# Start of an even layer's input projection: channel blocks transposed when due and modulated by ScalarE from PSUM instead of by GpSimd

## The chip, the cores and the metric

One core of a Trainium2 chip runs one program. The metric is device time in microseconds (us) of one execution. TensorE (PE) multiplies and transposes from SBUF into PSUM, VectorE (DVE), ScalarE (ACT) and GpSimd (POOL) work on tiles, and SP's queue issues most DMAs. Each engine runs its own instructions in its own order and waits at semaphores for the others.

## What is computed

The program is a two-layer backbone over 1024 latent tokens of width 1024, with a context of 256 tokens. Only the start of the first (even) layer matters here:

```python
h_lat = modulate(x, shift, scale)   # layer_norm(x) * (1 + scale) + shift
...
gq_l, gk_l, gv_l, glr_l, gg_l, cq_l, ckv_l, kr_l, mg_l = proj(h_lat)   # h_lat @ w_in
```

Shift and scale are rows of silu(c) @ ada_w + ada_b. All is float32. A matmul of two float32 operands is made of three matmuls in a shorter format: each operand is split into a high part (a cast) and a low part (the operand minus its high part), and the products high x high, high x low and low x high are added in PSUM.

## The kernel before

The projection wants h transposed: eight blocks j of 128 channels, each 1024 tokens wide, worked in two halves of 512 tokens (x tiles 0 to 3 and 4 to 7, of 128 tokens each). The function `startup` loads and normalises x tiles (`load_norm`: statistics on VectorE, L207; three small operations on GpSimd, L198, L199 and L214; the normalisation on ScalarE, L239), reduces the modulation weights to a column of shift and one of scale for each block (`modulation`, L248, on VectorE, two loads of 512 KB per block), and splits six weight tiles (`weight`: load L301, high part on ScalarE L302, low part L305 on VectorE, or on GpSimd for the weights numbered in `PLO`, 2 and 4).

Before the loop it transposes all eight blocks of the first half at once (L361) into eight PSUM banks. Block 0 is modulated from its bank by ScalarE (L321); the other seven are copied to SBUF tiles xnT (L368, five by ScalarE, two by VectorE) and modulated there by GpSimd when their turn comes (L323). `part` makes the high part of h on ScalarE (L328) and the low part on VectorE (L329). `products(t, j)` adds the three matmuls of weight tile t and block j into the accumulator of tile t (helper lines L146, L147, L148); six accumulators take six of the eight PSUM banks, the other two serve the rest.

The order in which the steps are issued is written out by hand in a string:

```python
ORDER = "m w w r m w w r m w r m m x r x x x r m C s r s m s s r s s s s"
```

Here m is one block's modulation columns, w a weight, r a first-half block (modulate, split, products), x an x tile of the second half, s a second-half block (transposes L350, modulation, split; the low part is put off to the next step that calls `catch_up`), and C prepares the evictions and the first step of the context. The framework beneath issues an instruction as soon as it expects its inputs and a free buffer, earlier in the program first, so that the engines' orders follow this string only roughly; on the chip each engine's order is then fixed.

After the loop the six accumulators are evicted (`dup_ev`, L517 on ScalarE and L519 on VectorE, for four tiles; other copies for two), and a generator `rest` makes the second-half products of the six tiles. `in_proj_a` weaves it with the context's preparation (`startup_ctx`: 16 more loads and reductions of modulation weights, transposes L423, splits) and then multiplies four of the kept weights with the context (matmuls named chi and clo, 256 columns wide). All SBUF tiles of this stage come from one pool of 48 buffers, so that a load waits until a buffer is free.

Of the kernel before, what the change touches and what calls it, by code (L numbers as in the profile page):

```python
# [12 lines left out]
F32 = mybir.dt.float32  # L13
F32R = mybir.dt.float32r
I32 = mybir.dt.int32
AF = mybir.ActivationFunctionType
ALU = mybir.AluOpType
# [3 lines left out]
P = 128  # L21
# [3 lines left out]
KD = D // P  # L25
# [6 lines left out]
def f32(ap):  # L32
    return ap.bitcast(F32)


class Weights:
# [9 lines left out]
    def next(self):  # L46
        self.fill(1 + self.ahead)
        return self.q.pop(0)
# [184 lines left out]
def load_norm(k, src):  # L233

    nc = k.nc
    xt = k.b4(name="xt")
    nc.sync.dma_start(xt, src)
    r, nm = k.ln_stats(xt)
    nc.scalar.activation(out=xt, in_=xt, func=AF.Identity, scale=r, bias=nm)  # L239
    return xt  # L240
# [12 lines left out]
def silu_rows(k, c):  # L253

    nc = k.nc
    row, o = k.b4(F32, (1, D), name="crow"), k.b4(name="cB")
    nc.sync.dma_start(row, c)
    k.act(row, row, AF.Silu)
    for s in range(0, D, 512):
        ps = k.bank()  # L260
        nc.tensor.matmul(ps, k.ones[0:1, :], row[:, s:s + 512], start=True, stop=True)
        nc.scalar.copy(out=o[:, s:s + 512], in_=ps)
    return o
# [3 lines left out]
T_CKV, T_KR, T_GK, T_GQ, T_CQ, T_GG, T_MG = 0, 1, 2, 4, 6, 8, 12  # L267
FIRST = (T_GQ, T_GQ + 1, T_GK, T_GK + 1, T_KR, T_CKV)


ORDER = "m w w r m w w r m w r m m x r x x x r m C s r s m s s r s s s s"
PLO, DVEV, REST_CONSTS = (2, 4), (2, 4), T_KR


def startup(k, context):


    nc, A = k.nc, k.A
    cB = silu_rows(k, A["c"])
    small = k.cpool.tile([P, 156], F32, name="small")  # L280
    nc.sync.dma_start(small, A["small"])
    k.sc, k.ab = small[:, 0:8], small[:, 8:24].rearrange("p (j w) -> p j w", w=2)
    k.m12, k.mlow = small[:, 24:88], small[:, 88:152].bitcast(I32)
    k.gng, k.mlag = small[:, 152:153], small[:, 153:156]
    xs = [load_norm(k, A["x"][i * P:(i + 1) * P, :]) for i in range(4)]

    nc.vector.tensor_scalar(out=k.ab[:, :, 1], in0=k.ab[:, :, 1], scalar1=1.0, scalar2=None, op0=ALU.add)
    tiles, ws, mods = FIRST, [], []
    h = ([], [])


    later = []

    def catch_up():
        while later:
            later.pop(0)()

    def weight():
        n = len(ws)
        raw, hi, lo = k.b4(F32, (P, KD, P), name="wraw"), k.b4(F32R, (P, KD, P), name="hi"), k.b4(F32R, (P, KD, P), name="lo")  # L300
        nc.sync.dma_start(raw, A["we"][tiles[n]])  # L301
        nc.scalar.copy(out=hi, in_=raw)  # L302
        ws.append((hi, lo))
        eng = nc.gpsimd if n in PLO else nc.vector
        eng.tensor_tensor(out=lo, in0=raw, in1=f32(hi), op=ALU.subtract)  # L305
        catch_up()
        for j in range(len(h[0])):
            products(n, j)

    def mod():  # L310
        j = len(mods)
        mods.append([])
        for w in range(2):
            mods[j].append(modulation(k, j, w, cB, f"mod{j}", nc.sync, 1))
            catch_up()

    def affine(out, in_, j):

        sh, sc = mods[j]
        if out is not in_:  # L320
            nc.scalar.activation(out=out, in_=in_, func=AF.Identity, scale=sc, bias=sh)  # L321
        else:
            nc.gpsimd.tensor_scalar(out=out, in0=in_, scalar1=sc, scalar2=sh, op0=ALU.mult, op1=ALU.add)  # L323

    def part(j, x, o):

        hi, lo = h[0][j][:, o:o + 512], h[1][j][:, o:o + 512]
        nc.scalar.copy(out=hi, in_=x)  # L328
        sub = lambda: nc.vector.tensor_tensor(out=lo, in0=x, in1=f32(hi), op=ALU.subtract)  # L329
        if o:  # L330
            later.append(sub)
            return
        sub()
        for t in range(len(ws) if acc else 0):
            products(t, j)

    def ready(j, x):
        for z in h:
            z.append(k.b4(F32R, name="h"))
        part(j, x, 0)  # L340

    def products(t, j):
        cnt[t] += 1
        k.mm3(acc[t], (ws[t][0][:, j, :], ws[t][1][:, j, :]), (h[0][j][:, :512], h[1][j][:, :512]), cnt[t] == 1, cnt[t] == KD)

    def second(j):

        ps = k.bank()
        for i in range(4):
            nc.tensor.transpose(ps[:, i * P:(i + 1) * P], xs[i][:, j * P:(j + 1) * P], k.ident)  # L350
        t = k.w2(name="x2")
        affine(t, ps, j)
        part(j, t, 512)

    cnt, acc = [0] * len(tiles), []
    mod()
    weight()
    ps = [k.bank() for _ in range(KD)]
    for i in range(4):
        for j in range(KD):  # L360
            nc.tensor.transpose(ps[j][:, i * P:(i + 1) * P], xs[i][:, j * P:(j + 1) * P], k.ident)  # L361
    x = k.w2(name="x2")
    affine(x, ps[0], 0)
    ready(0, x)
    xnT = [k.b4(F32, (P, 2, 512), name="xnT") for _ in range(KD // 2)]
    for j in range(1, KD):
        cp = nc.vector.tensor_copy if j in DVEV else nc.scalar.copy
        cp(out=xnT[j // 2][:, j % 2, :], in_=ps[j])  # L368
    k.act(k.sc, k.sc, AF.Silu)
    acc += [k.bank() for _ in tiles]  # L370
    products(0, 0)
    xs, sec = [], iter(range(KD))
    evac = None
    for e in ORDER.split():
        if e == "w":
            weight()
        elif e == "m":
            mod()
        elif e == "r":
            j = len(h[0])  # L380
            x = xnT[j // 2][:, j % 2, :]
            affine(x, x, j)
            ready(j, x)
        elif e == "x":
            i = 4 + len(xs)
            xs.append(load_norm(k, A["x"][i * P:(i + 1) * P, :]))
            catch_up()
        elif e == "s":
            second(next(sec))
        else:  # L390
            evac = even_state(k)
            next(context)
    catch_up()
    for n, t in enumerate(tiles):
        evac[t](acc[n], 0)
    k.keep = dict(zip(tiles, ws))

    def rest():
        for t in tiles:
            if t == REST_CONSTS:  # L400
                gla_consts(k)
            yield from k.proj_steps(k.keep[t], h, evac[t], first=512)
            if t in (T_GQ, T_GQ + 1):
                del k.keep[t]

    return h, rest()
# [1202 lines left out]
```

## Time and profile before

| | us |
|---|---|
| median of 3 runs | 1150.25 |
| lowest and highest | 1147.44, 1154.22 |
| the profiled execution | 1148.01 |
| its span, first to last instruction | 1146.2 |
| TensorE busy | 1091.3 |
| VectorE busy | 741.2 |
| ScalarE busy | 556.9 |
| GpSimd busy | 255.5 |

The span is a little shorter than the execution's time because the start and the end around the instructions aren't in it. Busy times are of one profiled execution; a matmul's end is modelled, since matmuls overlap in the array, and the time from one start to the next is the better measure of a run of them. PE is TensorE's matmuls, PEld its weight loads; L305 is line 305 of the kernel. The share of busy time is a mean over stages with different limits. The granted clock of 1.00 is 2.4 GHz, 0.50 is 1.2 GHz; a number between them is a mean over a stretch.

### The profile page before, as it was taken

The page shows a single profiled execution, that of the slowest core. Times are in us where ns is not written, and L with a number is a line of the kernel's source. Part 1 is how long each engine was busy: PE and PEld are TensorE (multiplying, and loading weights), DVE is VectorE, ACT ScalarE, POOL GpSimd, SP SyncE. Part 2 cuts the span into 40 slices and gives each one's busy share as a digit, 9 for nine tenths or more (in the row PEclk, how much of TensorE's full clock was granted, in tenths as well). Part 3 has the DMA queues.
Part 4 walks back from the last instruction along what each step waited for, and adds up shares of the span by engine and source line. Part 5 has one row for each costly group of instructions (what it writes and reads, how often), then busy time and mean ns, then how long its engine had stood idle before and what let it go on. Part 6 is the DMA issues. An engine that isn't in the chain of part 4 may idle for free.

```text
span 1146.2 us, 14541 instructions
## 1 busy us (share of the span) xinstructions
PE 1091.3 (95%) x5288; PEld 864.7 (75%) x5288; DVE 741.2 (65%) x1256; ACT 556.9 (49%) x956; POOL 255.5 (22%) x252
## 2 busy tenths in 40 slices
PE   5889999899999999999899999999999999999997
PEld 3668778778777777767677666888788888888885
DVE  6867684856655685776677677788526533664544
ACT  6285655576553367867677778313422223332000
POOL 3520000000000023323324366343101000022111
PEclk8989999999999999999999899999999999999999
DMA  9635562333535742213202424323400311125111
GB/s 373 244 129 195 204 225 100 130 119 126 194 121 164 255 131 52 46 25 88 69 3 49 125 74 135 123 110 134 160 1 1 111 37 55 55 71 202 59 55 55
DMA packets 41624, 131.88 MB, mean 115 GB/s; under 512 B 5545, under 2 KB 7337, under 8 KB 41554
## 3 DMA queue, kind: packets, MB, share of 16 engines
q1 hardware_dynamic: 35706, 114.81, 30.6%
q0 software_dynamic: 3056, 10.23, 2.3%
q10 hardware_dynamic: 2792, 5.94, 1.3%
q8 instruction: 41, 0.67, 0.3%
q14 instruction: 29, 0.24, 0.1%
HBM read 98.37 MB, written 20.36 MB: 104 GB/s over the span
## 4 chain that ended last, share of the span: by engine, by line
PE 76%; DVE 7%; ACT 6%; issue 3%; POOL 3%; DMA 3%; SPq 1%; POOLq 0%; DVEq 0%; ACTq 0%
PE ps L146 10%; PE ps L147 10%; PE ps L148 10%; PE pso L148 5%; PE pso L146 5%; PE pso L147 5%; PE pss L1068 3%; PE psm L993 3%; PE pss L1069 3%; PE pss L1070 3%; PE psav L1054 3%; PE psav L1053 3%; PE psav L1052 3%; PE psn L146 1%; PE psn L148 1%
## 5 line engine op out<-in xcount | busy, mean ns | idle before, releaser
L141 POOL TENSOR_TENSOR ph<-pexp,ph 128x512 fp32r<-128x512 f32 x80 | 108.3, 1359 | 175.8 <-ACT ph L136 143.4
L118 ACT ACTIVATE pexp<-pss 128x512 f32<-128x512 f32 x160 | 93.3, 596 | 63.4 <-PE pss L1070 61.7
L146 PE MATMUL ps<-h,hi 128*128 128x512 f32 x256 | 104.0, 418 | 5.6 <-ACT h L328 2.3
L994 DVE TENSOR_REDUCE mx<-psm 128x1 f32<-128x512 f32 (+1 forms) x192 | 102.3, 592 | 10.6 <-PE psm L993 10.4
L148 PE MATMUL ps<-h,lo 128*128 128x512 f32 x256 | 102.9, 402 | 3.1 <-DVE lo L305 1.8
L147 PE MATMUL ps<-h,hi 128*128 128x512 f32 x256 | 104.2, 407 | 0.8 <-DVE h L329 0.8
L141 DVE TENSOR_TENSOR ph<-pexp,ph 128x512 fp32r<-128x512 f32 x80 | 74.8, 940 | 44.4 <-ACT ph L136 42.7
L141 DVE TENSOR_TENSOR lo<-wraw,hi 128x1024 fp32r<-128x1024 f32 x37 | 47.1, 1283 | 85.3 <-ACT hi L136 80.3
L146 PE MATMUL pso<-hi,yh 128*128 128x512 f32 x256 | 99.8, 390 | 0.0
L147 PE MATMUL pso<-lo,yh 128*128 128x512 f32 x256 | 99.7, 390 | 0.0
L148 PE MATMUL pso<-hi,yl 128*128 128x512 f32 x256 | 99.0, 389 | 0.0
L136 ACT CAST ph<-pexp 128x512 fp32r<-128x512 f32 x160 | 95.2, 620 | 2.8
L146 PE MATMUL ps<-h1h,hi 128*128 128x512 f32 x192 | 75.1, 391 | 0.0
L148 PE MATMUL ps<-h1h,lo 128*128 128x512 f32 x192 | 74.7, 389 | 0.0
L147 PE MATMUL ps<-h1l,hi 128*128 128x512 f32 x192 | 74.7, 389 | 0.0
L1135 POOL TENSOR_TENSOR owr<-owr,rowB 128x1024 f32<-128x1024 f32 x16 | 42.4, 2659 | 119.8 <-DMA owr<-wo 119.8
L1054 PE MATMUL psav<-ph,V 128*96 128x512 f32 x160 | 63.8, 399 | 1.4 <-POOL ph L141 1.1
L1052 PE MATMUL psav<-ph,V 128*96 128x512 f32 x160 | 63.3, 396 | 0.2
L146 PEld LDWEIGHTS ps<-h,hi 128*128 128x128 f32 x256 | 48.9, 193 | 18.7 <-ACT h L328 3.9
L148 PEld LDWEIGHTS ps<-h,lo 128*128 128x128 f32 x256 | 49.1, 192 | 17.1 <-DVE lo L305 2.9
L147 PEld LDWEIGHTS ps<-h,hi 128*128 128x128 f32 x256 | 49.6, 194 | 11.5 <-issue 1.4
L148 PEld LDWEIGHTS pso<-hi,yl 128*128 128x128 f32 x256 | 48.0, 188 | 10.1
(358 smaller groups left out, 2590.0 us busy)
## 6 DMA issues: line engine op xcount, KB each, us to landing
aw<-ada SPq DMA_DIRECT2D x32, 512.0 KB, 9.0
araw<-ada SPq DMA_DIRECT2D x32, 512.0 KB, 3.6
wraw<-we SPq DMA_DIRECT2D x16, 512.0 KB, 4.6
owr<-wo SPq DMA_DIRECT2D x16, 512.0 KB, 4.8
xr<-x SPq DMA_DIRECT2D x16, 512.0 KB, 8.6
wraw<-wd SPq DMA_DIRECT2D x12, 512.0 KB, 4.1
xt<-x SPq DMA_DIRECT2D x8, 512.0 KB, 9.9
kt<-kn SPq DMA_DIRECT2D x16, 256.0 KB
```

The lines of the kernel that those rows point to most:

```text
L118: r = self.nc.scalar.activation(out=out, in_=in_, func=func, **kw)
L136: self.nc.scalar.copy(out=hi, in_=src)
L141: (lo_eng or self.nc.vector).tensor_tensor(out=lo, in0=src, in1=f32(hi), op=ALU.subtract)
L146: t.matmul(out, lhs[0], rhs[0], start=start, stop=False)
L147: t.matmul(out, lhs[0], rhs[1], start=False, stop=False)
L148: t.matmul(out, lhs[1], rhs[0], start=False, stop=stop)
L993: T.matmul(ps[:, :n], q[0][0:96, i * P:(i + 1) * P], cols(kt[0], s, n)[0:96], start=True, stop=True)
L994: nc.vector.reduce_max(out=mx[:, i, b:b + 1], in_=ps[:, :n], axis=AX.X)
L1052: T.matmul(a[0:96, :], vhi(j, hd), hi, start=j == 0, stop=False)
L1053: T.matmul(a[0:64, :], vlo(j, hd), hi, start=False, stop=False)
L1054: T.matmul(a[0:96, :], vhi(j, hd), lo, start=False, stop=j == NK - 1)
L1135: k.nc.gpsimd.tensor_tensor(out=raw, in0=raw, in1=k.ogate, op=ALU.mult)
```

## The change

GpSimd no longer modulates blocks nor subtracts weights. The transposes of a first-half block are issued when the block's turn comes, through the same function as those of the second half (`channels`), and ScalarE modulates from PSUM, for all 16 half blocks. All low parts of the start (weights and blocks) are put off into `later` and made by VectorE at the next `catch_up`. The accumulators take their banks before the first block. The order is another, the evictions (e) now stand in it between the second-half blocks, and the x tiles 0 to 7 are all kept to the end of the loop. The removed lines that stand in the kernel above are cut.

```diff
-ORDER = "m w w r m w w r m w r m m x r x x x r m C s r s m s s r s s s s"
-PLO, DVEV, REST_CONSTS = (2, 4), (2, 4), T_KR
+ORDER = "r w m r w m r w m r w m r w m r x m r x m r x x C s e s e s e s e s e s e s s"
+REST_CONSTS = T_KR
...
+    loaded = iter(tiles)
+
     def weight():
-        n = len(ws)
         raw, hi, lo = k.b4(F32, (P, KD, P), name="wraw"), k.b4(F32R, (P, KD, P), name="hi"), k.b4(F32R, (P, KD, P), name="lo")
-        nc.sync.dma_start(raw, A["we"][tiles[n]])
+        nc.sync.dma_start(raw, A["we"][next(loaded)])
         nc.scalar.copy(out=hi, in_=raw)
-        ws.append((hi, lo))
-        eng = nc.gpsimd if n in PLO else nc.vector
-        eng.tensor_tensor(out=lo, in0=raw, in1=f32(hi), op=ALU.subtract)
-        catch_up()
-        for j in range(len(h[0])):
-            products(n, j)
+
+        def low():
+            nc.vector.tensor_tensor(out=lo, in0=raw, in1=f32(hi), op=ALU.subtract)
+            ws.append((hi, lo))
+            for j in there:
+                products(len(ws) - 1, j)
+
+        later.append(low)
...
+    def channels(j, o):
+
+        if not o:
+            for z in h:
+                z.append(k.b4(F32R, name="h"))
+        ps = k.bank()
+        for i in range(4):
+            nc.tensor.transpose(ps[:, i * P:(i + 1) * P], xs[o // P + i][:, j * P:(j + 1) * P], k.ident)
         sh, sc = mods[j]
...
+        x = k.w2(name="x2")
+        nc.scalar.activation(out=x, in_=ps, func=AF.Identity, scale=sc, bias=sh)
         hi, lo = h[0][j][:, o:o + 512], h[1][j][:, o:o + 512]
         nc.scalar.copy(out=hi, in_=x)
...
+        def low():
+            nc.vector.tensor_tensor(out=lo, in0=x, in1=f32(hi), op=ALU.subtract)
+            if not o:
+                there.append(j)
+                for t in range(len(ws)):
+                    products(t, j)
+
+        later.append(low)
...
-    cnt, acc = [0] * len(tiles), []
+    cnt = [0] * len(tiles)
+    acc = [k.bank() for _ in tiles]
     mod()
+    k.act(k.sc, k.sc, AF.Silu)
     weight()
...
+    half = {0: iter(range(KD)), 512: iter(range(KD))}
+    evac, gone = None, iter(range(len(tiles)))
     for e in ORDER.split():
...
         elif e == "r":
+            channels(next(half[0]), 0)
         elif e == "x":
-            i = 4 + len(xs)
-            xs.append(load_norm(k, A["x"][i * P:(i + 1) * P, :]))
+            xs.append(load_norm(k, A["x"][len(xs) * P:(len(xs) + 1) * P, :]))
             catch_up()
         elif e == "s":
-            second(next(sec))
+            catch_up()
+            channels(next(half[512]), 512)
+        elif e == "e":
+            n = next(gone)
+            assert cnt[n] == KD
+            evac[tiles[n]](acc[n], 0)
         else:
+            catch_up()
             evac = even_state(k)
             next(context)
     catch_up()
-    for n, t in enumerate(tiles):
-        evac[t](acc[n], 0)
+    del xs[:]
     k.keep = dict(zip(tiles, ws))
```

## Rows read from the trace of the kernel before

**Rows 1.** The page: busy time, share of the span and instructions of each engine.
```profile
PE 1091.3 (95%) x5288; PEld 864.7 (75%) x5288; DVE 741.2 (65%) x1256; ACT 556.9 (49%) x956; POOL 255.5 (22%) x252
```
**Rows 2.** Busy time by stretch (us, length, engines with instruction counts, clock, DMA share, GB/s).
```profile
0.00:17.00 17.00, 9.33 (x36) 6.24 (x36) 8.46 (x21) 9.50 (x11) 6.78 (x18) 1.00 0.86 341
17.00:30.00 13.00, 7.92 (x16) 4.50 (x17) 10.86 (x13) 8.13 (x12) 3.93 (x2) 0.61 1.03 420
30.00:52.00 22.00, 19.37 (x81) 14.64 (x80) 17.96 (x29) 4.67 (x6) 10.80 (x11) 1.00 0.77 292
52.00:64.00 12.00, 7.64 (x37) 5.59 (x37) 5.77 (x12) 8.74 (x12) 5.44 (x9) 0.87 0.00 0
64.00:77.00 13.00, 12.47 (x50) 9.63 (x50) 9.13 (x18) 10.84 (x15) 5.07 (x7) 0.86 0.41 142
77.00:125.00 48.00, 47.37 (x266) 40.82 (x264) 35.95 (x61) 29.75 (x56) 3.03 (x5) 1.00 0.60 210
```
**Rows 3.** The same by stretch for the second matmul of a product (L147) alone.
```profile
0.00:64.00 64.00, 15.39 (x36) 0.90 0.70 276
64.00:77.00 13.00, 5.66 (x13) 0.86 0.41 142
```
**Rows 4.** Waits of GpSimd and of ScalarE up to 80 us: total, times, longest.
```profile
POOL xnT L323 <- DVE mod L248: 21.8, 5, 9.1
...
ACT h L328 <- POOL xnT L323: 20.4, 5, 5.5
```
**Rows 5.** Timeline around 25 us (start, us, engine, line, operation, idle before).
```profile
25.00 2.37 POOL L305 TENSOR_TENSOR lo<-wraw,hi 128x1024 fp32r<-128x1024 f32 x1
...
25.71 2.21 DVE L329 TENSOR_TENSOR h<-xnT,h 128x512 fp32r<-128x512 f32 x1 [1.32 <-ACT h L328]
```
**Rows 6.** Timeline: second-half transposes begin; the last first-half low part.
```profile
57.31 0.44 PE L350 MATMUL ps<-ident,xt 128*128 128x128 f32 x2 [1.82 <-ACT xt L239]
...
75.30 0.69 DVE L329 TENSOR_TENSOR h<-xnT,h 128x512 fp32r<-128x512 f32 x1 [1.24 <-ACT h L328]
```
**Rows 7.** Timeline: the first statistics of x, which wait for its load.
```profile
5.46 1.29 DVE L207 BATCH_NORM_STATS2 bnst<-xt 128x6 f32<-128x512 f32 x2 [2.26 <-DMA xt<-x]
```
**Rows 8.** Groups by line up to 125 us: busy, mean ns, idle before.
```profile
L248 DVE CUSTOM_DVE_ANT_0 aw<-aw,cB,small 128x1024 f32<-128x1024 f32 x16 | 19.8, 1274 | 0.0
...
L329 DVE TENSOR_TENSOR h<-x,h 128x512 fp32r<-128x512 f32 x9 | 6.1, 687 | 8.8 <-ACT h L328 8.8
...
L305 DVE TENSOR_TENSOR lo<-wraw,hi 128x1024 fp32r<-128x1024 f32 x4 | 4.9, 1219 | 4.2 <-ACT hi L302 4.2
...
L517 ACT ACTIVATE dup<-ps 64x512 f32<-64x512 f32 x24 | 14.0, 592 | 7.0 <-PE ps L148 5.8 <-DVE dup L519 1.0
L239 ACT ACTIVATE xt<-xt,nm,rstd 128x1024 f32<-128x1024 f32 x10 | 12.4, 1243 | 8.8 <-POOL nm L214 8.4
L321 ACT ACTIVATE x<-ps,mod,mod 128x512 f32<-128x512 f32 x9 | 6.7, 779 | 1.6 <-PE ps L350 1.2 <-PE ps L361 0.4
...
L328 ACT CAST h<-x 128x512 fp32r<-128x512 f32 x9 | 5.4, 621 | 0.0
```
**Rows 9.** Timeline of TensorE: transposes, full-width products, half-width products, the last of these.
```profile
69.83 1.03 PE L350 MATMUL ps<-ident,xt 128*128 128x128 f32 x8
...
85.32 0.39 PE L146 MATMUL ps<-h,hi 128*128 128x512 f32 x1
...
86.00 0.39 PE L146 MATMUL ps<-h,hi 128*128 128x512 f32 x1
...
118.21 0.28 PE L146 MATMUL ps<-chi,hi 128*128 128x256 f32 x1
118.33 0.28 PE L147 MATMUL ps<-clo,hi 128*128 128x256 f32 x1
...
122.51 0.28 PE L148 MATMUL ps<-chi,lo 128*128 128x256 f32 x1
```
**Rows 10.** Waits of SP's queue up to 125 us: total, times, longest.
```profile
SPq L246 <- PE ps L350: 32.3, 1, 32.3
```

More of the change, by code (lines that the diff above doesn't have):

```diff
@@ L287, in startup @@
     nc.vector.tensor_scalar(out=k.ab[:, :, 1], in0=k.ab[:, :, 1], scalar1=1.0, scalar2=None, op0=ALU.add)
-    tiles, ws, mods = FIRST, [], []
+    tiles, ws, mods, there = FIRST, [], [], []
     h = ([], [])
@@ L315, in mod @@
             catch_up()
-    def affine(out, in_, j):
-        sh, sc = mods[j]
[L320 to L325, printed above, removed]
+    def channels(j, o):
[5 more added lines that the diff above has]
+            nc.tensor.transpose(ps[:, i * P:(i + 1) * P], xs[o // P + i][:, j * P:(j + 1) * P], k.ident)
+        sh, sc = mods[j]
+        x = k.w2(name="x2")
+        nc.scalar.activation(out=x, in_=ps, func=AF.Identity, scale=sc, bias=sh)
         hi, lo = h[0][j][:, o:o + 512], h[1][j][:, o:o + 512]
         nc.scalar.copy(out=hi, in_=x)
[L329 to L340, printed above, removed]
+        def low():
[5 more added lines that the diff above has]
+        later.append(low)
     def products(t, j):
@@ L344, in products @@
         k.mm3(acc[t], (ws[t][0][:, j, :], ws[t][1][:, j, :]), (h[0][j][:, :512], h[1][j][:, :512]), cnt[t] == 1, cnt[t] == KD)
[L346 to L353, printed above, removed]
-    cnt, acc = [0] * len(tiles), []
+    cnt = [0] * len(tiles)
+    acc = [k.bank() for _ in tiles]
     mod()
+    k.act(k.sc, k.sc, AF.Silu)
     weight()
[L358 to L373, printed above, removed]
+    half = {0: iter(range(KD)), 512: iter(range(KD))}
+    evac, gone = None, iter(range(len(tiles)))
     for e in ORDER.split():
@@ L379, in startup @@
         elif e == "r":
[L380 to L383, printed above, removed]
+            channels(next(half[0]), 0)
         elif e == "x":
-            i = 4 + len(xs)
-            xs.append(load_norm(k, A["x"][i * P:(i + 1) * P, :]))
+            xs.append(load_norm(k, A["x"][len(xs) * P:(len(xs) + 1) * P, :]))
             catch_up()
         elif e == "s":
-            second(next(sec))
+            catch_up()
[4 more added lines that the diff above has]
+            evac[tiles[n]](acc[n], 0)
         else:
+            catch_up()
             evac = even_state(k)
```

## The prediction

> **What bounds the kernel now.** I first read the busy time by engine over the whole span: TensorE is busy 95% of 1146.2 us [rows 1]. A change of the start can then only give back time in which TensorE waits there. So I next cut the first 125 us into stretches [rows 2]. From 77 us on TensorE has no gap: 47.37 of 48 us at full clock. Before that it has gaps: 7.9 of 13 us busy between 17 and 30, at half clock for much of it (0.61 mean), and 7.6 of 12 between 52 and 64. The DMA share is 1.03 (420 GB/s) from 17 to 30 and zero from 52 to 64, so loads limit only the first 50 us or so.
>
> How much first-half work is done shows in the count of one of the three matmuls of each product [rows 3]: 36 products of the 48 (six tiles by eight channel blocks) by 64 us, and 49 by 77 us, that is all 48 and one of the second half. The waits tell who is late [rows 4]: ScalarE's cast of h waits 20.4 us for GpSimd's modulation (L323), which itself waits 21.8 us for the modulation columns of VectorE. GpSimd also slows VectorE: while its subtraction of a weight runs 2.37 us, VectorE's subtraction of h takes 2.21 us [rows 5], and without such a neighbour 0.69 [rows 6]. Last, the order: at 57.31 us transposes of the second half still wait for a normalised x [rows 6], and the low part of the eighth first-half block comes at 75.30 us, long after the loads (none from 52 to 64 us).
>
> **The change, part by part.** All durations are of the profiled execution (span 1146.2 us, 1148.01 us in all); the median of three runs is 1150.25 us, 2.2 us above it. I subtract the gain from the median.
>
> *Loads.* The same 30 pieces of 512 KB; at 420 GB/s one takes 1.25 us. x0 is there at 5.46 us [rows 7], the tenth piece (end of the second modulation pair) 9 x 1.25 later, at 16.7 us; the x7 piece at 5.46 + 29 x 1.25 = 41.8 us. No queue but SP's issues them, before and after.
>
> *VectorE.* Seven steps of the new order each need two reductions of modulation weights (1.27 each), one low part of h (0.69) and, for five of them, one low part of a weight (1.22) [rows 8]: 4.45 us. GpSimd's two weight subtractions come to VectorE (2 x 1.22), its two copies into xnT go, and so do the 1.5 us by which a subtraction of h was stretched beside each of the two: about even. From 16.7 us the steps end at 21.2, 25.6, 30.1, 34.5, 39.0; then x4 (1.29 for its two statistics [rows 7]), the seventh pair at 43.5, x5, the eighth at 48.1, x6, the last low part at 50.1, x7 at 51.4 us. VectorE has no slack there, and the old order needed until 75.3 us for the same low part [rows 6].
>
> *ScalarE.* Eight modulations from PSUM at 0.78 take the place of one plus five copies to xnT: 5.5 us more modulation than before and 3 us fewer copies, in stretches where it was busy 4.67 of 22 us [rows 2]. I cost it at nothing; in the worst case it adds its own 1.4 us (modulation and cast) once, behind the last pair, which is in the 50.1 us above.
>
> *TensorE, first half.* The low part of a weight makes its products ready 3.2 us into a step: 2 products at 19.9, 4 at 24.3, 6 at 28.8, 8 at 33.2, 10 at 37.7, then 6 each at 41.0, 45.5 and 50.1 us. A product is three matmuls at a start-to-start of 0.227 us, 0.68 us [rows 9]. From 28.8 us on this is a queue that never empties: 6 + 8 + 10 + 18 products, 28.6 us, end at 57.4 us. The transposes, 0.5 us for a block of four (two blocks in 1.03 us [rows 9]), no longer lie in the empty start: seven blocks, of which three fit in the gaps before 28.8, add 2.0. End of the first half: 59.5 us, and not at 76 us as now. Bounds: 2 us earlier if the high-part matmuls go ahead of the low parts, 0.7 later if 17 to 30 us is at half clock again (the four products of 24.3 us then take 5.4 us and end at 29.7).
>
> *Second half.* x7's statistics end at 51.4; GpSimd's chain (ten normalisations waited 8.4 us for it, 0.84 each at the least [rows 8]; I take 1.5), ScalarE's normalisation (1.24), a transpose block (0.5), modulation 0.78, cast 0.62, subtraction 0.69 make the first block ready near 57 us, inside the first half's queue; the chain may take 2 us more before it shows. Then ScalarE sets the pace: eight times 1.40, and between them the evictions of the six accumulators, now issued there: eight copies of 0.59 for four tiles, three more like them for the other two. 17.7 us from 55, so the eighth block is ready near 73 us. If TensorE can take any opened tile, a step of 2.58 us feeds it one product per free bank: it starves only in the first two steps, for 2.5 us. Bounds: 0, and 4.9 us if it keeps to one tile until 73 us (13.7 us less seven products, 4.8, and eight transpose blocks, 4.0).
>
> *Sum.* From 59.5: 48 products 32.6, transposes 4.0, the context's 96 half-width matmuls at 0.12 [rows 9] 11.5, its transposes 2.0, value products in between 0.9: 51.0. With 2.5 lost, the last context product ends at 113.0 us. Now it ends at 122.8 us [rows 9]. The same sum from 77 us of before (47 products, context, values: 46.4) gives 123.4, 0.6 too late, so the method holds. The gain is 9.8 us. Later stages are TensorE's (95%), so it should be kept; their order may shift by 3 us either way. Forecast: 1150.25 - 9.8 = 1140.5 us, with 1136 to 1144 for this case alone.
>
> **Rivals.**
>
> *More gain.* High parts first, transposes all in gaps, nothing lost in the second half: 9.8 + 2 + 2 + 2.5, about 16 us, 1134 us. For it: before 30 us the gaps are there [rows 2]. Against: it needs every bound at its good end.
>
> *The clock falls.* The granted clock was 0.61 on average after a stretch of transposes and waits, and 0.87 and 0.86 around 52 to 77 us [rows 2], where TensorE waited; it is 1.00 once it is full. The new second half mixes transposes and short bursts on a few banks. If it ran at 1.2 instead of 2.4 GHz from 59.5 to 73 us, half of that work, 6.6 us, would be pushed on: 1147 us. Against: the queue of the first half leaves TensorE full just before. The Trainium skill (TensorE: Matmul & The Clock Gate, section "A second HAM failure mode: psum-queue depth-cycling") says that cycling through PSUM banks can make short idle times that let the clock swing between its two levels. By that rule this rival would be the rule and not the exception; the rows show the fall only behind waits of several us.
>
> *The context chain decides (slower).* SP's load of the context's modulation weights waited 32.3 us for the last second-half transposes [rows 10], which end at 70.9 us [rows 9] and hold the x buffers; from there to the last context product it is 51.9 us. The change keeps all eight x tiles to the end of the second half. If those 52 us are a chain of their own, the end follows the last transposes, which come near 71.5 us by the pace above: 123.4 us, 0.6 us more than now, 1151 us. If the stretch starts as late against the first half as now (4.4 of the 12 us from 52 to 64 lost [rows 2]), 5 us more: 1156 us. It decides a loss of over 0.5% from 76.4 us for the last transposes. Against it: TensorE has no gap from 77 us on [rows 2], so that today the matmuls are the bound and not this chain; and x0 to x3 may come free at 45 us, sooner than now.
>
> *The moved work is hidden anyway.* It would be if TensorE had been full in 17 to 64 us; it was busy 35 of 47 us there, some of it at half clock, so this has no share of its own.
>
> **How the numbers follow.** About 0.5% (5.75 us) is what a measurement of this kernel can tell from no change: faster is below 1144.5 us, slower above 1156. Forecast 0.57 (nearly all of it faster), more gain 0.15, clock 0.14 (a third faster, the rest the same), context chain 0.14 (half the same, half slower). Faster 0.72, same 0.21, slower 0.07. The range runs from the more-gain case and its 1 us of noise, 1133, to the milder end of the context case, 1150.
>
> **What would show it.** Right: no modulation on GpSimd; no wait of ScalarE's cast for GpSimd; VectorE full from 17 to 50 us; the last first-half low part near 50 us; TensorE without gaps from about 29 us but for some 2.5 us near 60; the last context product at 111 to 115 us; the rest of the span unchanged in length. Wrong: a low clock between 55 and 75 us, context loads that start at 71 us or later with TensorE idle behind them, or a first half that ends later than 62 us; also if the gain is there at 125 us and is lost again by a later stage.

## The result, and the profile after

| | before | after |
|---|---|---|
| median (range, runs) | 1151.2 us (1147.44 to 1154.22, 4) | 1167.41 us (1166.36 to 1169.09, 4) |
| ratio, 95% interval | | 1.0143 [1.0114, 1.0171] |
| profiled execution, its span | 1148.01, 1146.2 us | 1167.44, 1165.7 us |
| second matmul of a product (L147) up to 64 us, 64 to 77 us | 36, 13 [rows 3] | 37, 12 |
| end of the last context product | 122.8 us [rows 9] | 141.7 us |
| span behind it | 1023.4 us | 1024.0 us |

One L147 of the kernel after runs across the mark at 64 us and is counted on both sides of it. The kernel is slower by 16 us, where 9.8 us less had been forecast. All of it is lost in the start: the last context product comes 18.9 us later, and what follows it takes as long as before in these two profiled executions. I read the page's busy line first, then the stretches (columns as in [rows 2]) and the same for L147 alone.

```profile
PE 1096.3 (94%) x5288; PEld 865.6 (74%) x5288; DVE 739.3 (63%) x1256; ACT 559.6 (48%) x958; POOL 241.5 (21%) x243
```

```profile
17.00:30.00 13.00, 9.03 (x25) 5.98 (x26) 9.70 (x13) 4.94 (x7) 0.00 (x0) 0.87 1.03 420
30.00:52.00 22.00, 17.45 (x79) 13.73 (x78) 12.98 (x18) 7.04 (x9) 0.00 (x0) 1.00 0.78 294
...
64.00:77.00 13.00, 10.52 (x37) 7.54 (x37) 7.76 (x16) 4.67 (x6) 4.81 (x7) 0.87 0.26 81
77.00:100.00 23.00, 14.77 (x51) 10.97 (x52) 15.69 (x26) 20.58 (x31) 4.17 (x10) 0.55 0.25 86
100.00:125.00 25.00, 25.00 (x116) 20.51 (x115) 13.31 (x25) 15.88 (x30) 0.31 (x1) 1.00 0.61 200
```

```profile
0.00:64.00 64.00, 15.47 (x37) 7.49 (x37) 0.97 0.71 276
64.00:77.00 13.00, 5.37 (x12) 2.46 (x12) 0.87 0.26 81
77.00:100.00 23.00, 3.30 (x6) 1.79 (x7) 0.55 0.25 86
```

The work did move: GpSimd has nothing from 17 to 52 us, where it was busy 14.7 us [rows 2]. But TensorE got nothing for it. It has finished 36 products by 64 us, as before, and 48 by 77 us, one fewer than before, and between 30 and 52 us it is busy less (17.45 us against 19.37 [rows 2]). VectorE, which the prediction had full in that stretch, is busy 12.98 of 22 us. Then comes the loss: between 77 and 100 us only six L147, at a granted clock of 0.55, where TensorE had had 23.00 us of work at 1.00.

The waits up to 150 us (total, times, longest) say who is late in the first half:

```profile
ACT x L330 <- PE ps L327: 21.7, 6, 6.7
DVE h L335 <- ACT h L332: 20.5, 8, 4.5
ACT xt L239 <- POOL nm L214: 15.3, 6, 5.4
...
PE ps L146 <- ACT h L332: 9.5, 7, 2.3
```

GpSimd's late modulation [rows 4] is gone, and three waits stand in its place: ScalarE's modulation waits for the transposes, VectorE's low part waits for ScalarE, TensorE's products wait for ScalarE. One step of the timeline shows that they are one ring:

```profile
43.98 0.60 PE L327 MATMUL ps<-ident,xt 128*128 128x128 f32 x4
...
44.62 0.78 ACT L330 ACTIVATE x<-ps,mod,mod 128x512 f32<-128x512 f32 x1 [5.36 <-PE ps L327]
45.42 0.62 ACT L332 CAST h<-x 128x512 fp32r<-128x512 f32 x1
...
46.08 0.69 DVE L335 TENSOR_TENSOR h<-x,h 128x512 fp32r<-128x512 f32 x1 [3.15 <-ACT h L332]
...
46.10 1.42 PE L146 MATMUL ps<-h,hi 128*128 128x512 f32 x5 [1.52 <-ACT h L332]
...
48.17 1.28 DVE L248 CUSTOM_DVE_ANT_0 aw<-aw,cB,small 128x1024 f32<-128x1024 f32 x1
...
49.37 1.28 DVE L248 CUSTOM_DVE_ANT_0 aw<-aw,cB,small 128x1024 f32<-128x1024 f32 x1
...
53.04 1.03 PE L327 MATMUL ps<-ident,xt 128*128 128x128 f32 x8
53.67 0.78 ACT L330 ACTIVATE x<-ps,mod,mod 128x512 f32<-128x512 f32 x1 [6.68 <-PE ps L327]
...
55.13 0.69 DVE L335 TENSOR_TENSOR h<-x,h 128x512 fp32r<-128x512 f32 x1 [4.47 <-ACT h L332]
```

At 50.65 us both reductions of the next block are done (49.37 plus 1.28). Its transposes need x, which is long there, and one of the two spare PSUM banks, the last of which ScalarE's modulation has read by 45.40 us; yet they stand in TensorE's queue behind the products of the block before and run at 53.04. The modulation follows at 53.67. VectorE's next instruction is the low part of that block, so VectorE stands idle for 4.47 us with the next reductions queued behind. The pairs of reductions start at 27.18, 34.02, 40.43, 48.17, 57.25 and 65.22 us: steps of 6.4 to 9.1 us, and not 4.45.

The rest of the loss is in the timeline of TensorE and of ScalarE behind the first half, whose last matmul ends at 75.47 us (75.08 plus 0.39):

```profile
75.08 0.39 PE L148 MATMUL ps<-h,lo 128*128 128x512 f32 x1
77.31 0.44 PE L327 MATMUL ps<-ident,xt 128*128 128x128 f32 x2 [1.84 <-ACT xt L239]
79.67 0.69 PE L327 MATMUL ps<-ident,xt 128*128 128x128 f32 x2 [1.92 <-ACT xt L239]
...
90.73 1.12 PE L327 MATMUL ps<-ident,xt 128*128 128x128 f32 x4 [1.27 <-ACT dup L498]
92.53 0.79 PE L146 MATMUL ps<-h,hi 128*128 128x512 f32 x1 [0.68 <-ACT x L330]
93.12 0.63 PE L147 MATMUL ps<-h,hi 128*128 128x512 f32 x1
93.55 0.63 PE L148 MATMUL ps<-h,lo 128*128 128x512 f32 x1
```

```profile
76.01 1.24 ACT L239 ACTIVATE xt<-xt,nm,rstd 128x1024 f32<-128x1024 f32 x1
78.37 1.24 ACT L239 ACTIVATE xt<-xt,nm,rstd 128x1024 f32<-128x1024 f32 x1 [1.12 <-POOL nm L214]
80.18 1.44 ACT L330 ACTIVATE x<-ps,mod,mod 128x512 f32<-128x512 f32 x2 [0.56 <-PE ps L327]
...
85.94 1.24 ACT L239 ACTIVATE xt<-xt,nm,rstd 128x1024 f32<-128x1024 f32 x1 [0.53 <-POOL nm L214]
...
88.31 1.24 ACT L239 ACTIVATE xt<-xt,nm,rstd 128x1024 f32<-128x1024 f32 x1
```

For 17.1 us (75.47 to 92.53) TensorE has transposes and no product. x6 and x7 are normalised only at 76.01 and 78.37 us; behind them ScalarE modulates, casts, evicts and normalises the context's two tiles (85.94, 88.31) in turn. The first product of the second half (92.53) stands in TensorE's queue behind the transposes of all eight second-half blocks (the last at 90.73), 5.5 us after the low part of the first block is done on VectorE:

```profile
86.43 0.63 DVE L335 TENSOR_TENSOR h<-x,h 128x512 fp32r<-128x512 f32 x1
```

Before, these transposes ran from 52 us on (57.31 in [rows 6] is not the first of them) and were over at 70.86 us [rows 9], while the first half still waited for its last block (to 75.30 us) [rows 6], and products of the second half filled that wait:

```profile
71.30 0.50 PE L146 MATMUL ps<-h,hi 128*128 128x512 f32 x1 [0.43 <-ACT x L321]
```

The second half was prepared in the first half's waits, and five of its products ran there.

### The profile page after: what moved, and what is told of

Its sections match the earlier page's. It is cut to its first block, busy times and chain, and to the rows that moved or that the text cites. A ratio compares the mean times of both kernels' runs of the same rounds, so it can differ in the third digit from the quotient of the medians.

```text
span 1165.7 us, 14547 instructions
## 1 busy us (share of the span) xinstructions
PE 1096.3 (94%) x5288; PEld 865.6 (74%) x5288; DVE 739.3 (63%) x1256; ACT 559.6 (48%) x958; POOL 241.5 (21%) x243
## 4 chain that ended last, share of the span: by engine, by line
PE 77%; DVE 7%; ACT 6%; DMA 4%; issue 3%; POOL 2%; SPq 0%; POOLq 0%; DVEq 0%; ACTq 0%
PE ps L146 11%; PE ps L147 11%; PE ps L148 11%; PE pso L147 5%; PE pso L148 5%; PE pso L146 5%; PE psm L974 3%; PE pss L1049 3%; PE pss L1050 3%; PE pss L1051 3%; PE psav L1035 2%; PE psav L1034 2%; PE psav L1033 2%; DMA araw<-ada 1%; PE psn L146 1%
## 5 line engine op out<-in xcount | busy, mean ns | idle before, releaser
L146 PE MATMUL ps<-h,hi 128*128 128x512 f32 x256 | 105.6, 423 | 12.8 <-ACT h L332 9.5
L975 DVE TENSOR_REDUCE mx<-psm 128x1 f32<-128x512 f32 (+1 forms) x192 | 102.4, 590 | 11.0 <-PE psm L974 10.7
L147 PE MATMUL ps<-h,hi 128*128 128x512 f32 x256 | 105.3, 412 | 0.0
L147 PE MATMUL pso<-lo,yh 128*128 128x512 f32 x256 | 99.7, 390 | 0.0
L147 PE MATMUL ps<-h1l,hi 128*128 128x512 f32 x192 | 74.7, 389 | 0.0
L198 POOL TENSOR_SCALAR rstd<-bnmv 128x1 f32<-128x1 f32 x34 | 21.3, 626 | 184.3 <-DVE bnmv L1151 110.1
L147 PEld LDWEIGHTS ps<-h,hi 128*128 128x128 f32 x256 | 50.0, 195 | 11.1 <-issue 1.4
```

Source lines behind the costliest of these rows:

```text
L146: t.matmul(out, lhs[0], rhs[0], start=start, stop=False)
L147: t.matmul(out, lhs[0], rhs[1], start=False, stop=False)
L975: nc.vector.reduce_max(out=mx[:, i, b:b + 1], in_=ps[:, :n], axis=AX.X)
```

## The experiments

Three theories. **E**: the new engines cost this themselves (ScalarE's modulations, VectorE's two more subtractions). **T**: the order of the first half's queues strings it out; at first this meant only the transposes behind the products of the block before, later (**V**) also the low part right behind its own reductions. **S**: the second half, emitted only behind the first, is what is late.

All ratios are against the kernel before, run in the same sessions.

| run | median (range, runs), us | ratio, interval | last context product, us |
|---|---|---|---|
| after | 1167.41 (1166.36 to 1169.09, 4) | 1.0143 [1.0114, 1.0171] | 141.7 |
| before_scalar_modulates | 1151.13 (1146.1 to 1154.63, 10) | 1.0002 [0.9981, 1.0023] | 123.1 |
| tail_order_back | 1162.9 (1160.66 to 1164.14, 4) | 1.0094 [1.0069, 1.0119] | 132.9 |
| evictions_last | 1166.71 (1163.54 to 1169.63, 4) | 1.0129 [1.0098, 1.0159] | 139.5 |
| x_early | 1164.17 (1161.11 to 1165.76, 4) | 1.0116 [1.0089, 1.0144] | 134.7 |
| low_at_once | 1170.14 (1168.65 to 1172.84, 4) | 1.0174 [1.0146, 1.0202] | 140.5 |
| transposed_ahead | 1160.2 (1157.87 to 1163.95, 5) | 1.0079 [1.0053, 1.0105] | 135.0 |
| ahead_and_tail_2 | 1157.76 (1153.19 to 1161.52, 10) | 1.0053 [1.0034, 1.0073] | 131.6 |
| reductions_ahead | 1163.13 (1162.2 to 1164.47, 4) | 1.0101 [1.0074, 1.0129] | 137.0 |
| reductions_and_transposes_ahead | 1152.29 (1149.9 to 1154.26, 10) | 1.0003 [0.9986, 1.002] | 126.0 |
| all_three | 1155.65 (1149.5 to 1157.34, 12) | 1.0032 [1.0016, 1.0048] | 127.4 |
| context_norms_last | 1164.02 (1160.58 to 1165.42, 5) | 1.0097 [1.0072, 1.0122] | 134.8 |
| evictions_earlier | 1156.8 (1150.32 to 1158.42, 11) | 1.0045 [1.0025, 1.0065] | 129.4 |
| evictions_last_2 | 1153.82 (1150.15 to 1155.57, 11) | 1.0027 [1.0011, 1.0044] | 125.3 |

**E: the engines alone.** before_scalar_modulates keeps the order of before and lets ScalarE do all modulations and VectorE all weight subtractions:

```
-PLO, DVEV, REST_CONSTS = (2, 4), (2, 4), T_KR
+PLO, DVEV, REST_CONSTS = (), (2, 4), T_KR
...
-            nc.gpsimd.tensor_scalar(out=out, in0=in_, scalar1=sc, scalar2=sh, op0=ALU.mult, op1=ALU.add)
+        nc.scalar.activation(out=out, in_=in_, func=AF.Identity, scale=sc, bias=sh)
```

> The kernel before with all modulations on ScalarE (from the xnT tiles) and all low parts of weights on VectorE, order and transposes as before. Theory E: slower than before by 5 us or more, 1156 us and up. Theories S and T: the engines that do it are not what costs, 1143 to 1152 us; faster by some us if GpSimd's shared time with VectorE and its longer modulation were on the path.

Measured: no difference (1.0002, interval within 0.23%). E falls, as far as the order of before can show it. The engine move gains nothing by itself either, although it takes away the slow subtractions beside GpSimd [rows 5].

**S: the order of the second half.** Three runs move its parts in the changed kernel's order string, and one takes the delay of the low parts out.

```
-ORDER = "r w m r w m r w m r w m r w m r x m r x m r x x C s e s e s e s e s e s e s s"
tail_order_back
+ORDER = "r w m r w m r w m r w m r w m x x x x r m C s r s m s s r s s s s e e e e e e"
evictions_last
+ORDER = "r w m r w m r w m r w m r w m r x m r x m r x x C s s s s s s s s e e e e e e"
x_early
+ORDER = "r w m r w m x r w m x r w m x r w m x r m r m r C s e s e s e s e s e s e s s"
low_at_once
-        later.append(low)
+        low()
```

> The changed kernel's functions and the front of its order, but x4 to x7 and the second-half blocks woven among the last three first-half blocks as in the kernel before, evictions last. Theory S (the second half is prepared only behind the first, so that TensorE has no products for 17 us after 75 us): most of the loss goes, 1148 to 1156 us, and the product-free gap is under 5 us. Theory T (each block's transposes stand in TensorE's queue behind the products of the block before, which strings out the first half): that loop is untouched, 1162 us or more. Theory E (ScalarE's modulations and VectorE's extra low parts are themselves what costs): 1162 us or more.

> The changed kernel with the six evictions behind the eight second-half blocks, nothing else. Theory S, if what delays the second-half blocks is x6 and x7 coming late: 1164 to 1168 us, hardly better. If it is the copies of the evictions, which stand between the blocks on ScalarE and hold TensorE's transposes: about 6 us less, 1159 to 1162 us. Theory T: 1167 us, no change.

> The changed kernel with x4 to x7 loaded and normalised between the weights instead of between and behind the last blocks. If what makes the second half late is the x tiles' chain (VectorE, GpSimd, ScalarE) that stands behind the first half and, twice, ahead of a block's modulation on ScalarE: the waits of ScalarE for GpSimd (15.3 us) nearly go, second-half transposes start when the first half ends, and the whole takes 1156 to 1161 us. If the pace of ScalarE and of two PSUM banks in the second half is what costs: 1164 us or more. Theory T alone expects 1165 us or more, as the loads of the weights come later.

> The changed kernel with each low part issued right behind its high part instead of at the next catch-up, so only this piece of the order of low parts undone. Theories S and T: the low parts are not what is late, 1164 to 1170 us. A rival, that putting them off behind the next reduction is what strings out the steps (VectorE waited 20.5 us for casts): 1160 us or less.

Measured: putting the second half's x tiles and blocks among the last first-half steps gives 4.5 us of the 16 back (1167.41 to 1162.9); theory S had expected 1148 to 1156, and 1162.9 lies where T and E had it. The evictions between the blocks are worth nothing that can be told. x_early shortens the 17 us without products to 5.2 (74.08 to 79.25; TensorE is busy 12.47 of 13 us from 64 to 77) but starves the first half (13.95 of 22 us from 30 to 52 instead of 17.45); 3 us come back. Calling the low parts at once does not help either (1.0174). So S is a part and not the whole.

**T: the transposes.** transposed_ahead emits the transposes of first-half block j+1 right behind block j's, before the products of block j:

```
+    ahead = []
+
+    def transposed(j, o):
+        ps = k.bank()
+        for i in range(4):
+            nc.tensor.transpose(ps[:, i * P:(i + 1) * P], xs[o // P + i][:, j * P:(j + 1) * P], k.ident)
+        return ps
...
+        ps = ahead.pop() if ahead else transposed(j, o)
...
+        if not o and j + 1 < KD:
+            ahead.append(transposed(j + 1, 0))
```

> The changed kernel with the transposes of a first-half block issued one block earlier, into the second spare PSUM bank. Theory T: ScalarE no longer waits for them (21.7 us of waits now), the first half ends some 9 us before 75 us, and the whole takes 1156 to 1160 us. Theory S: the first half may end earlier, but the gap before the second half widens by as much, 1163 to 1167 us.

Measured: 7 us back (1160.2). The first half ends at 69.6 us, and 17.1 us without products still lie behind it (to 86.70). VectorE's timeline now has a step that repeats to the hundredth:

```profile
32.94 1.28 DVE L248 CUSTOM_DVE_ANT_0 aw<-aw,cB,small 128x1024 f32<-128x1024 f32 x1
...
36.99 0.69 DVE L343 TENSOR_TENSOR h<-x,h 128x512 fp32r<-128x512 f32 x1 [1.55 <-ACT h L340]
37.94 1.23 DVE L306 TENSOR_TENSOR lo<-wraw,hi 128x1024 fp32r<-128x1024 f32 x1 [0.26 <-ACT hi L303]
39.09 1.28 DVE L248 CUSTOM_DVE_ANT_0 aw<-aw,cB,small 128x1024 f32<-128x1024 f32 x1
```

6.15 us from pair to pair (32.94 to 39.09): the work and two waits, 1.55 and 0.26 us. The first is the low part, which stands directly behind the reductions that its own modulation needs; the next pair is queued behind it. That is theory V, formed here.

The transposes ahead and the tail of tail_order_back were then put together. In the first kernel for it, ahead_and_tail, blocks 0 and 1 of the second half took the first half's blocks 6 and 7 that lay transposed ahead: the same instructions, but these two blocks then hold other rows and channels of x. It took 1157.42 us (1152.22 to 1162.32, 10 runs), 1.0054 [1.0032, 1.0076], last context product 129.1. In all_early (the same edit with the order "r w m r w m x r w m x r w m x r w m x r m C s s r m s s r s s s s e e e e e e") it was blocks 0 and 2: 1157.03 us (1155.29 to 1164.18, 6 runs), 1.0063 [1.0034, 1.0092], 131.6. ahead_and_tail_2 is ahead_and_tail with the second half transposing its own (`if ahead and not o` in the edit above), and the later kernels that transpose ahead do the same.

> Both undone at once: transposes one block ahead, and the second half woven among the last first-half blocks with the evictions last. If the serial loop through TensorE's queue (7 us, from transposed_ahead) and the late second half (4.5 us, from tail_order_back) are separate losses, they add: 1154 to 1157 us, the last context product near 128 us. If they are one loss seen twice, no better than the better one: 1159 to 1161 us.

> All that theories S and T name undone: transposes one block ahead, x tiles between the weights, second-half blocks woven among the last first-half blocks, evictions last. If the two theories hold all of the loss, it is back at or under the kernel before, 1145 to 1153 us, with TensorE without a gap of over 2 us from 37 us on. If 1156 us or more, something else of the change costs, of which the two spare PSUM banks are the next suspect.

> The two undone parts together, as in ahead_and_tail, with the second half's blocks transposed for themselves: the first half's transposes one block ahead, and the second half's x tiles and blocks put among the last steps of the first half as the kernel before had them. In ahead_and_tail a block of the second half took the block of the first half that had been transposed ahead (its numbers were those of other rows), with the same instructions. S and T together: 1153 to 1159, last context product at 127 to 131 us, and 5 us or so remain above the kernel before. If the swapped blocks had changed the order of the waits: anything from 1150 to 1163.

Measured: all three leave about 6 us of loss. S and T do not explain it all.

**V: the reductions.** One "m" more at the front of the order puts the pair of block j+1 ahead of the low part of block j. reductions_ahead does that alone, reductions_and_transposes_ahead does both, all_three weaves the second half in as well:

```
-ORDER = "r w m r w m r w m r w m r w m r x m r x m r x x C s e s e s e s e s e s e s s"
reductions_ahead, reductions_and_transposes_ahead
+ORDER = "m r w m r w m r w m r w m r w m r x m r x r x x C s e s e s e s e s e s e s s"
all_three
+ORDER = "m r w m r w m r w m r w m r w x m x r x x m C s r s s r s s s s s e e e e e e"
```

> The changed kernel with one thing moved: the two reductions of block j+1 stand ahead of the low part of block j in VectorE's queue (one more 'm' at the front of the order). Theory V: a low part that stands right behind its own reductions makes VectorE wait for ScalarE's modulation and cast at every step (1.55 us where the transposes are early, more where they are late), so that its step is 6.1 us and more where its work is 4.45; with the next reductions between, the waits go. V alone: steps of 4.6 to 5.5 us, first half over by 64 to 70 us, 1157 to 1163. Theory T (the transposes behind the products of the block before are what strings the first half out): ScalarE waits for TensorE's transposes as long as before (15 to 22 us in all), the steps stay at 6 us and more, 1163 to 1168.

> Both the reductions and the transposes one block ahead, with the changed kernel's late second half. V and T together: VectorE's step 4.4 to 4.8 us, first half over at 60 to 63 us (the 59.5 that the prediction had), 69.2 in transposed_ahead; but the second half is still prepared behind it, so that TensorE has 12 to 17 us without products after it: last context product 129 to 134 us, 1153 to 1159. If VectorE's order is worth nothing beside the transposes: as transposed_ahead, 1159 to 1162.

> Reductions and transposes one block ahead, and the second half's x tiles and blocks woven into the last steps of the first half, evictions last. If S, T and V are all there is: TensorE has no stretch of over 3 us without products between 30 us and the last context product, which ends at 120 to 126 us (122.8 before): 1146 to 1153, no slower than the kernel before. If something else of the change still costs (ScalarE's evictions, VectorE's extra low parts): 1154 to 1159, as ahead_and_tail.

Measured: alone, 4 us (1163.13), at the border between the two expectations. The pairs start 5.9 to 7.7 us apart up to 50.6 us, and ScalarE waits for the transposes even longer (from 18 to 130 us; 21.1 us in the changed kernel):

```profile
ACT x L330 <- PE ps L327: 27.4, 6, 6.7
```

Both together give 15 of the 16 us back (1152.29; 1.0003), more than the 7 and the 4 of each alone and more than was expected (1153 to 1159): either wait alone keeps the ring closed. VectorE, then the stretches, of reductions_and_transposes_ahead:

```profile
36.02 1.28 DVE L248 CUSTOM_DVE_ANT_0 aw<-aw,cB,small 128x1024 f32<-128x1024 f32 x1
...
38.44 0.68 DVE L343 TENSOR_TENSOR h<-x,h 128x512 fp32r<-128x512 f32 x1
40.36 1.23 DVE L306 TENSOR_TENSOR lo<-wraw,hi 128x1024 fp32r<-128x1024 f32 x1 [1.24 <-ACT hi L303]
41.50 1.28 DVE L248 CUSTOM_DVE_ANT_0 aw<-aw,cB,small 128x1024 f32<-128x1024 f32 x1
```

```profile
30.00:52.00 22.00, 21.59 (x96) 16.70 (x95) 17.60 (x27) 6.73 (x10) 0.00 (x0) 1.00 0.79 296
52.00:64.00 12.00, 12.00 (x56) 9.89 (x55) 8.10 (x16) 7.29 (x8) 7.04 (x13) 1.00 0.24 88
64.00:77.00 13.00, 5.93 (x33) 4.65 (x32) 7.27 (x13) 11.29 (x18) 2.36 (x6) 0.71 0.00 0
```

The low part of h waits for nothing any more, and TensorE is full from 30 to 64 us: the queue that the prediction had. The step is 5.48 us (36.02 to 41.50), over the 4.4 to 4.8 expected: the weight's low part now waits 1.24 us for its high part, which stands on ScalarE behind the modulation. The first half ends at 64.7 us, the first product of the second half comes at 78.23. The first half ends 10.7 us earlier than in the changed kernel, and the time without a product behind it is 13.5 us and not 17.1. The kernel before has no such hole: its first half ended near 80 us, with five products of the second half already done. What the end at 64.7 us gains against it is given back in the hole, and the time is that of before and not below (the last context product ends at 126.0 us, 3.2 later than before).

all_three moves that hole forward and gains nothing (1.0032). TensorE's timeline:

```profile
58.61 0.47 PE L325 MATMUL ps<-ident,xt 128*128 128x128 f32 x1 [2.48 <-ACT xt L239]
60.79 0.47 PE L325 MATMUL ps<-ident,xt 128*128 128x128 f32 x1 [1.70 <-ACT xt L239]
```

Here the second half's transposes stand in TensorE's queue ahead of the first half's last blocks and wait for x, whose statistics in turn put the last reductions off: with those of all four x tiles ahead of it the last pair starts at 55.92 us, with only x4's (reductions_and_transposes_ahead) at 52.09. The time lies where the expectation put a remaining cost of the engines, but the cause is an order again: TensorE has transposes alone from 55.5 to 69.1 us, 13.5 us again.

**What holds the hole open.** On reductions_and_transposes_ahead: the context's load and normalisations behind the second half's blocks (a new letter N for what C did second), then also the evictions one block earlier, then all evictions behind the blocks.

```
 reductions_and_transposes_ahead
-ORDER = "m r w m r w m r w m r w m r w m r x m r x r x x C s e s e s e s e s e s e s s"
 context_norms_last
+ORDER = "m r w m r w m r w m r w m r w m r x m r x r x x C s e s e s e s e s e s e s s N"
 evictions_earlier
+ORDER = "m r w m r w m r w m r w m r w m r x m r x r x x C e s e s e s e s e s e s s s N"
 evictions_last_2
+ORDER = "m r w m r w m r w m r w m r w m r x m r x r x x C s s s s s s s s e e e e e e"
```

> reductions_and_transposes_ahead with the context's load, silu and two normalisations emitted after the second half's blocks. If they hold the second half (they stand in ScalarE's queue at 67.4, 71.8 and 74.0 us and wait there for GpSimd): the first product of the second half comes at 70 to 73 us instead of 76.0, last context product 121 to 124, 1147 to 1151. If the evictions and the x tiles hold it: first product at 74 to 77 us, 1150 to 1154.

> As context_norms_last, with each first-half accumulator evicted one block of the second half earlier. If the PSUM banks hold the transposes of the second half: first product of the second half at 69 to 72 us, up to 2 us under context_norms_last, 1146 to 1150. If they do not: within 1 us of context_norms_last.

> reductions_and_transposes_ahead with all evictions behind the second half's eight blocks, the context's normalisations left where they are. If evictions between the blocks cost more than the banks they free: first product of the second half at 72 to 75 us, 1149 to 1152. If the banks decide: the first product needs an evicted accumulator's bank and comes later, at 77 to 82 us: 1153 to 1159.

Measured: two misses, and one that doesn't decide. In context_norms_last the first product of the second half does come earlier, at 74 us, and the kernel is still 12 us slower than reductions_and_transposes_ahead. TensorE's timeline shows the context's transposes, which now wait in its queue among the products:

```profile
82.97 0.63 PE L146 MATMUL ps<-h,hi 128*128 128x512 f32 x1
89.99 0.47 PE L413 MATMUL ps<-ident,xt 128*128 128x128 f32 x1 [6.40 <-ACT xt L239]
```

evictions_earlier has its first product at about the same time and gets 7 us of that back, where under 2 had been expected; there the first normalisation of the context runs on ScalarE at 83.15 us and not at 88.70, and TensorE has no such wait. In evictions_last_2 the first product comes at 76.5 us, 1.8 us earlier than with the evictions in between and not later, but at 1153.82 us the time is not lower; its range overlaps the other's. (The 76.0 us of the expectations, for the first product of reductions_and_transposes_ahead, is the start of the last transposes; the product comes at 78.23.) So with the context's normalisations moved the hole is still 9.8 us long, with the evictions moved 12.3, and neither alone closes it. What lies in it is to be seen in TensorE's timeline of reductions_and_transposes_ahead:

```profile
64.57 1.03 PE L325 MATMUL ps<-ident,xt 128*128 128x128 f32 x8
66.36 1.32 PE L325 MATMUL ps<-ident,xt 128*128 128x128 f32 x8 [0.76 <-ACT x L336]
70.16 1.97 PE L325 MATMUL ps<-ident,xt 128*128 128x128 f32 x8 [2.47 <-ACT x L336]
75.95 1.97 PE L325 MATMUL ps<-ident,xt 128*128 128x128 f32 x8 [3.83 <-ACT dup L506]
78.23 0.80 PE L146 MATMUL ps<-h,hi 128*128 128x512 f32 x1 [0.31 <-ACT x L336]
```

These are the transposes of all eight second-half blocks, two blocks at a time because two PSUM banks are spare, and between them TensorE waits 7.1 us in all for ScalarE to empty a bank. Only then comes the first product, since the program emits the second half's products (`rest`) behind all eight blocks. The first products of the changed kernel (92.53 behind 90.73), of evictions_last_2 (76.45 behind 75.68) and of the kernel before (71.30 behind 69.83 [rows 9]) stand behind the last transposes in the same way; before, the first half's last blocks still had products to do meanwhile. An order with products between these transposes was not tried, so that it would close the hole is not shown. No kernel tried is faster than the one before.

## Why the prediction was wrong

The method of the sum held: the rest of the span kept its length, and the time followed the last context product. What failed were three steps, all in one way: work per engine was added up as if each instruction could start when its operands were there. The last context product came 28.7 us after the forecast 113.0. By the sum's own terms that is 16.0 us for the first half (75.5 and not 59.5), 10.6 for the start of the second (17.1 us without products, less the 2.5 and the 4.0 of transposes that the sum had) and about 2.6 for 13 matmuls behind it (92.53 to 98.24, granted clock 0.50, 0.43 us apart and not 0.227): 29.2, an estimate from these rows.

- *VectorE*, "Seven steps of the new order each need ... 4.45 us", "VectorE has no slack there". The busy time was right: two reductions at 1.28 and subtractions at 0.69 and 1.22 are what the trace of after has. The waits were missing. Its queue has the low part of block j behind the reductions of block j, and ScalarE's modulation (0.78) and cast (0.62) lie between them: with the transposes early 1.55 us in every step that has a weight, a step of 6.15 (transposed_ahead); 6.4 to 9.1 as it was. In the program the low parts of a block are called between the two reductions of the next block; in VectorE's queue they came out ahead of both (46.08, then 48.17 and 49.37 above). The prediction costed that chain "once, behind the last pair"; it recurs in every step.
- *TensorE, first half*, "a queue that never empties", transposes put in gaps. The gaps were no place for them: block j+1's transposes came behind block j's products in TensorE's queue, which made ScalarE wait 21.7 us in all. The first half ended at 75.5 us and not 59.5. With both orders mended TensorE is full from 30 to 64 us and the first half ends at 64.7, so the step was right about the work and wrong about the order. Its "not at 76 us as now" misread the kernel before: of the 49 L147 by 77 us, five are products of the second half, and those of the last first-half block end near 80 us. The sum is not touched by it (47 products are left either way), but it hid that the old order filled its last wait with the second half.
- *Second half*, first block "near 57 us, inside the first half's queue". The modulation of its first blocks came at 80.18 us, its first low part at 86.43, its first product at 92.53; 17.1 us without products, where 2.5 were forecast. That a step "feeds it one product per free bank" failed: no product ran between the blocks, because the products stand behind the transposes of all eight, and these wait for banks. The statistics of x stand behind the late reductions on VectorE, the evictions and the context's normalisations between the blocks on ScalarE.
- *ScalarE*, costed at nothing: right for its busy time (before_scalar_modulates: 1.0002), wrong for its place. It is a link between VectorE and itself, and the delay is VectorE's.
- *Loads* held. From 17 to 30 us the DMA moves 420 GB/s, as before, and no later wait of the first half that is shown above ends on a load.

Of the rivals, *the context chain decides* had the sign and not the mechanism. Its 51.9 us from the second half's last transposes to the last context product would give 143.8 us from their end at 91.85 (90.73 plus 1.12, the last L327 of TensorE's timeline), and 141.7 was measured. But SP's wait for these transposes was shorter than before, not longer [rows 10], and from 100 us to 125 TensorE is full:

```profile
SPq L246 <- PE ps L327: 23.4, 1, 23.4
```

So what follows the transposes is for the most part TensorE's own work (the sum's 32.6 + 11.5 + 2.0 + 0.9 = 47.0 us of the 49.8), and the transposes were late because the first half and x were. *The clock falls* was a consequence: the mean is 0.55 from 77 to 100 us, behind waits, and the matmuls start 0.43 us apart (93.12 to 93.55) instead of 0.227. The Trainium skill (TensorE: Matmul & The Clock Gate, "A second HAM failure mode: psum-queue depth-cycling"), which the prediction named, describes a kernel that cycles through PSUM banks and whose short idle times come often enough for the clock to swing between its two levels. The profile of after doesn't show that from 30 to 52 us: there TensorE cycled through banks and stood idle about 1.5 us in each step, and the granted clock was 1.00. *The moved work is hidden anyway* was given no share, and it is what before_scalar_modulates shows for the engines alone (1.0002).

## What to carry to other kernels

Adding up what each engine has to do gives the time only where its queue is in the right order. For each instruction that is moved, read what stands directly ahead of it and behind it on its own engine, and whether a result has to go to another engine and back between two neighbours; such a pair pays the round trip in every step unless work of the next step is put between. Two such pairs in one ring are worth opening together: here each alone gave 7 and 4 us, both gave 15. And where a kernel has idle time in one phase, ask which other phase fills it before making the first one shorter.

## What the runs showed of the hardware

The span behind the last context product was 1021.3 to 1029.3 us in the profiled executions of these kernels and of the one before, and in none of them between 1024.0 and 1026.6, although none of the edits touches that part. The difference doesn't go with the kernel's start, and it is of the size of the spread within one kernel (1146.1 to 1154.63 us in before_scalar_modulates); its cause is open.
